# Expert rows fetched, added and stored instead of accumulated by the DMA, with two experts' weights loaded after the first gathers

## The chip, the cores and the metric

The kernel runs on one core of a Trainium2 chip. The metric is the device time of one execution in microseconds (us), as the median of several runs. A profile is taken of one execution, and its times count from the start of that execution's span.

## The reference, cut to what matters

The program computes one layer of a streaming encoder for 1024 frames of a prompt and 64 frames of a sample (1088 rows of 1024 fp32 values). After two kinds of attention and an output projection, every row goes through a mixture of 32 experts, of which each row uses two, both out of one of four groups:

```python
x = x + merge_branches(o_a, o_b, gate_logit, w_pa, w_pb, w_o)
hx = rmsnorm(x, g_ffn)
grp = argmax(hx @ w_rg + b_rg)
top_p, top_i = top_k(softmax(fine_sel), 2)
expert = grp * 8 + top_i
hid = silu(hx @ w1[e]) * (hx @ w3[e]) * combine[e]
x = x + sum_e hid @ w2[e]
```

The weights of an expert are w1 and w3 (1024 x 128) and w2 (128 x 1024), all fp32: three loads of 512 KB.

## The kernel before

The program is one long list of instructions for each engine. The last quarter of it is what matters here: the output projection (`out` and `out_tile`, nine tiles of 128 rows) and the experts (`moe`).

**Output projection.** Each tile of rows is multiplied by w_o and added to the input rows in a tile `y`. The result goes to the output `out_y` in DRAM (line 927), its normalized copy goes to a DRAM buffer `hxd` (line 934), and a router (`route`, `place`) works out which slot of which expert each row takes. An expert has 96 slots (`CAP`). Slots that no row takes get a row number far outside the buffer. The router's last result is `ptab`, a table of slots by experts, held in PSUM.

**Experts.** `moe` takes them in an order in which the group changes at every step (`expert`), so two experts that can share a row are at least four steps apart. For each expert it

- gathers up to 96 normalized rows from `hxd` by an indirect DMA on GpSimd's queue (`gather`, line 1066); an unfilled slot moves nothing,
- transposes them on TensorE (`turn`), multiplies by w1 and w3 and applies silu (`hidden`),
- multiplies by w2 into two PSUM halves, which ScalarE (left half, line 1112) and VectorE (right half, line 1114) scale by the row's weight into a tile `ot`, and adds `ot` onto the rows of `out_y` by an indirect DMA that accumulates in DRAM (`scatter`, line 1115). All 96 slots are moved there: an unfilled slot adds to one of 4 x 96 spare rows behind the real ones (line 1128 works out their numbers).

The gathers run up to `XG` = 3 experts ahead, the transposes two, `hidden` one.

**Weights.** `prefetch` (line 1054) issues the loads on SyncE's queue as soon as three free 4 KB-wide buffers (`units`) are there, at most `PF` = 3 loads in flight. There are 37 such buffers, 12 experts' worth. Seven experts' weights are loaded during the output projection, as tiles of the projection come free. After it, 16 more units are free, 8 called "r" and 8 called "u":

```python
self.free.extend(("r" * 8 + "u" * 8)[:NU0])
self.prefetch()
self.drain()
self.close("rp")
self.mp = self.open("mp", 1)
self.free.extend(("r" * 8 + "u" * 8)[NU0:])
```

With `NU0` = 8 the eight r units are handed out before the router's work drains; with the rest `moe` starts at step `E0` = -1, where it calls `prefetch` again. `HOLD_G` = -1 makes the first load that is issued there wait for the third gather. Later loads follow as experts finish.

**End.** `overflow` counts, after the last expert, how many experts have more than 96 rows (lines 1167 to 1184), and all engines branch on that number. With these inputs no expert has.

**Order.** TensorE's order is the order of the code. The order on the other engines, and on SyncE's and GpSimd's queues, is set by a scheduler.

Of the kernel before, what the change touches and what calls it, by code (L numbers as in the profile page):

```python
# [9 lines left out]
F32 = mybir.dt.float32  # L10
F32R = mybir.dt.float32r
BF = mybir.dt.bfloat16
I32 = mybir.dt.int32
U32 = mybir.dt.uint32
AF = mybir.ActivationFunctionType
OP = mybir.AluOpType
# [3 lines left out]
D = 1024  # L20
NTOK = 1088
NT = 9
NEG = -1e30
BIG = 1.0e6
CAP = 96
NOV = 22
EPS = 1e-6
NBIG, NSMALL = 4, 4
O_TURN, O_LOG, O_RANK, O_TAB = 3, 4, 7, 3
SA, SB, PTA, PTB, NORM_POOL, D_NORM, ATT0, ATT1, WPOOL, WR, SS, WO_EVERY, PF, SQ, V_POOL, RC_ACT, KT, NX, NN, NU0, E0, YB = 4, 3, 2, 1, 2, 0, 2, 26, 0, 4, 1, 3.5, 3, 2, 2, 2, 1, 10, 1, 8, -1, 3  # L30
PA, PF2, HOLD_G, HELD, WARM0, XG, OT, HXB = 8, 2, -1, 1, 11, 3, 2, 1
FIRST, GRP0 = 0, 4
WARM = 6, 3, 0, 2, 14
S_LOAD, S_H, S_H2, S_W, S_V, S_EVERY, GB = 4.5, 1.5, 6.5, 5.0, 3, 24, 2
# [8 lines left out]
def rows(i):  # L43
    return 128 if i < 8 else 64


class K:
# [1033 lines left out]
    def hidden(self, u, xT):  # L1081
# [16 lines left out]
        nc.vector.tensor_tensor(hl, t, hh.bitcast(F32), op=OP.subtract)  # L1098
        return (hh, wh), (hh, wl), (hl, wh)

    def scatter(self, parts, idx_r, wcol):

        nc = self.nc
        ot = self.mp.tile([128, D], F32, name="ot", bufs=OT)
        for hf in range(2):
            sl = slice(512 * hf, 512 * hf + 512)
            po = self.pp.tile([128, 512], F32, name="big", bufs=NBIG)
            for j, (a, b) in enumerate(parts):
                self.mm(po[:CAP], a, b[:, sl], start=(j == 0), stop=(j == 2))
            o = ot[:CAP, sl]  # L1110
            if hf == 0:
                nc.scalar.activation(o, po[:CAP], AF.Copy, scale=wcol)  # L1112
            else:
                nc.vector.tensor_scalar(o, po[:CAP], wcol, None, op0=OP.mult)  # L1114
        return nc.gpsimd.indirect_dma_start(out=self.O["y"], out_offset=bass.IndirectOffsetOnAxis(ap=idx_r, axis=0),  # L1115
                                     in_=ot[:CAP], in_offset=None, bounds_check=NTOK + 4 * CAP - 1, compute_op=OP.add)

    def moe(self):
        nc = self.nc

        t = self.mp.tile([CAP, 32], F32, name="t2")
        ti = self.mp.tile([CAP, 2, 32], I32, name="ti")
        tw = self.mp.tile([CAP, 32], F32, name="tw")
        self.placed = nc.vector.tensor_scalar(ti[:, 0], self.ptab[:, 0], BIG, None, op0=OP.add)
        nc.scalar.activation(tw, self.ptab[:, 1], AF.Copy, scale=0.5)
        for j in range(4):
            g = slice(8 * j, 8 * j + 8)
            nc.vector.tensor_scalar(t[:, g], self.ptab[:, 2, g], self.spare_b[:CAP, j:j + 1],
                                    self.spare[:CAP, j:j + 1], op0=OP.mult, op1=OP.add)
        nc.vector.tensor_tensor(ti[:, 1], self.ptab[:, 0], t, op=OP.add)  # L1130

        self.xgs = xgs = self.y[-XG:]
        xT, parts, sc = {}, {}, []
        for e in range(-XG, 32):
            if e + XG < 32:
                x = self.expert(e + XG)
                g = self.gather(ti[:, 0, x:x + 1], xgs[e % XG])
                if e == HOLD_G:
                    self.hold = g
            if e == E0:  # L1140
                self.prefetch()
            for d in (1, 2) if e < 0 else (2, 1):
                if d == 1 and 0 <= e + 1 < 32:
                    parts[e + 1] = self.hidden(self.ew[e + 1], xT.pop(e + 1))
                if d == 2 and 0 <= e + 2 < 32:
                    xT[e + 2] = self.turn(xgs[(e + 2) % XG])
            if e >= 0:
                x = self.expert(e)
                st = self.scatter(parts.pop(e), ti[:, 1, x:x + 1], tw[:, x:x + 1])
                for y in self.sy if e < 4 else sc[-4:-3]:  # L1150
                    self.after(st, y)
                for y in sc[-3:]:
                    self.tc.declare_no_dep(st.ins, y.ins, reason="a frame has one group; rows of another")
                sc.append(st)
                self.free.extend(self.which[e])
                self.prefetch()

    def overflow(self):

        nc, tc, I = self.nc, self.tc, self.I  # L1160
        V = nc.vector
        p = self.mp

        def T(name, *shape, dt=F32):
            return p.tile([128, *shape], dt, name=name, bufs=1)
        self.placed = None
        pc = self.pp.tile([128, 32], F32, name="small", bufs=NSMALL)
        for j in range(2):
            self.mm(pc, self.onesb, self.ohs[:, j], start=(j == 0), stop=(j == 1))
        nov = T("nov", 32)  # L1170
        V.tensor_scalar(nov, pc, float(CAP), None, op0=OP.is_gt)
        for m in range(2, (NTOK - 1) // CAP + 1):
            V.scalar_tensor_tensor(nov, pc, float(CAP * m), nov, op0=OP.is_gt, op1=OP.add)  # L1173
        inc = [T("inc0", 32), T("inc1", 32)]
        V.tensor_copy(inc[0], nov)
        a = 0
        for d in (1, 2, 4, 8, 16):
            V.tensor_copy(inc[1 - a][:, :d], inc[a][:, :d])  # L1178
            V.tensor_tensor(inc[1 - a][:, d:], inc[a][:, d:], inc[a][:, :32 - d], op=OP.add)  # L1179
            a = 1 - a  # L1180
        inc = inc[a]
        tot = T("tot", 1, dt=I32)
        V.tensor_copy(tot, inc[:, 31:32])
        val = nc.values_load(tot[0:1, 0:1], min_val=0, max_val=NOV)
        with tc.If(val > 0):
            ovb = T("ovb", 32)
            V.tensor_tensor(ovb, inc, nov, op=OP.subtract)
            fill = T("ofill", NOV, 3)
            V.memset(fill, 0.0)
# [1 line left out]
            for i in range(NT):  # L1191
                n = rows(i)
                for j in range(2):
                    jk, b, m, r = T("ojk", 32), T("ob", 1), T("om", 1), T("orow", 1, dt=I32)
                    V.scalar_tensor_tensor(jk[:n], self.ie[:n], self.ep[:n, i, j, 0:1], ovb[:n],
                                           op0=OP.is_equal, op1=OP.mult, accum_out=b[:n])
                    pos = self.ep[:n, i, j, 1:2]
                    V.tensor_scalar(m[:n], pos, float(CAP), BIG, op0=OP.is_lt, op1=OP.mult)
                    V.tensor_tensor(m[:n], m[:n], pos, op=OP.add)
                    V.tensor_scalar(b[:n], b[:n], float(CAP), -float(CAP), op0=OP.mult, op1=OP.add)  # L1200
                    V.tensor_tensor(r[:n], b[:n], m[:n], op=OP.add)
                    nc.gpsimd.indirect_dma_start(
                        out=self.otable, out_offset=bass.IndirectOffsetOnAxis(ap=r[:n, 0:1], axis=0),
                        in_=self.ent[:n, i, j, :], in_offset=None, bounds_check=CAP * NOV - 1, oob_is_err=False)
# [3 lines left out]
            w3v = I["w3"][0].rearrange("e (p k) f -> (e p) (k f)", k=8)  # L1208
            w2v = I["w2"][0].rearrange("e f d -> (e f) d")
            with tc.For_i(0, val):  # L1210
                jk, e, ix = T("ojk", 32), T("oe", 2), T("oix", 2, dt=I32)
                V.tensor_scalar(jk, inc, num, None, op0=OP.is_le)
                V.tensor_reduce(e[:, 0:1], jk, axis=mybir.AxisListType.X, op=OP.add)
                V.tensor_copy(e[:, 1:2], num)
# [4 lines left out]
                for dst, src in zip(u, (w1v, w3v, w2v)):  # L1219
                    nc.gpsimd.indirect_dma_start(  # L1220
                        out=dst, out_offset=None, in_=src,
                        in_offset=bass.IndirectOffsetOnAxis(ap=ix[:, 0:1], axis=0), bounds_check=4095, oob_is_err=False)
                ob = T("otb", 3)
                nc.gpsimd.indirect_dma_start(
                    out=ob[:CAP], out_offset=None, in_=self.otable,
                    in_offset=bass.IndirectOffsetOnAxis(ap=ix[:CAP, 1:2], axis=0), bounds_check=CAP * NOV - 1, oob_is_err=False)
                ti, tr, tw = T("oti", 2, dt=I32), T("otr", 1), T("otw", 1)
# [189 lines left out]
```

## Time and profile before

| what | value |
| --- | --- |
| median of 3 runs | 1236.51 us (1236.01 to 1240.26) |
| the profiled execution | 1243.3 us, of which the span is 1241.5 us |
| busy in the span | PE 1187.3 us (96%), VectorE 801.4 us (65%), ScalarE 741.1 us (60%), GpSimd 319.2 us (26%) |
| moved by DMA | 156.32 MB, of which the queue of GpSimd (q0) 21.50 MB |

The profiled execution is 6.8 us longer than the median of the runs. PE is TensorE's matmuls, DVE is VectorE, ACT is ScalarE, POOL is GpSimd, SP is SyncE. The DMA share is the mean busy share of the core's 16 DMA engines; it can pass 1, as packets of two queues overlap on an engine. q1 is the queue of SyncE, q10 that of ScalarE, q0 that of GpSimd's indirect DMAs.

### The profile page before, as it was taken

How to read it: one execution, taken by the hardware profiler on the slowest of the kernel's cores; microseconds unless marked ns; L12 is line 12 of the kernel's file. 1: busy time of each engine (PE TensorE's matmuls, PEld its weight loads, DVE VectorE, ACT ScalarE, POOL GpSimd, SP SyncE). 2: the span in 40 equal slices, each digit the busy share in tenths (PEclk: the TensorE clock that was granted, in tenths of full speed). 3: DMA queues.
4: the chain of work that ended last, by engine and by line, in shares of the span. 5: the costliest groups of instructions: out<-in, count | busy, mean ns of one | idle time of the engine just before them, and what ended most of it. 6: DMA issues, size and time to landing. Idle time of an engine off the chain costs nothing. (4 is left out here: it accounts for less than half of the span.)

```text
span 1241.5 us, 22308 instructions
## 1 busy us (share of the span) xinstructions
PE 1187.3 (96%) x7605; PEld 1105.8 (89%) x7605; DVE 801.4 (65%) x2476; ACT 741.1 (60%) x1730; POOL 319.2 (26%) x469
## 2 busy tenths in 40 slices
PE   8999999999999999999999899999999989999884
PEld 6899999999889999999898899999888859999773
DVE  6768776767498888978467685229544445655443
ACT  5789998989598988988456444324233323333221
POOL 2644435352434334100000000000000024554321
PEclk9999999999999999999999899999999989999887
DMA  8113121312222231411234333214674479999995
GB/s 283 56 55 92 33 74 50 90 48 78 58 82 56 70 67 40 88 44 43 67 89 131 88 89 99 59 45 143 230 264 154 136 215 268 287 282 282 283 280 136
DMA packets 102539, 156.32 MB, mean 126 GB/s; under 512 B 13581, under 2 KB 77941, under 8 KB 102389
## 3 DMA queue, kind: packets, MB, share of 16 engines
q1 hardware_dynamic: 92789, 124.43, 33.1%
q0 software_dynamic: 7168, 21.50, 8.0%
q10 hardware_dynamic: 2464, 8.91, 1.8%
q8 instruction: 61, 1.00, 0.3%
q14 instruction: 57, 0.47, 0.1%
HBM read 122.08 MB, written 38.23 MB: 129 GB/s over the span
## 5 line engine op out<-in xcount | busy, mean ns | idle before, releaser
L83 PE MATMUL big<-w,hTh 128*128 128x384 f32 (+1 forms) x1152 | 322.8, 351 | 0.9 <-ACT raw L380 0.3
L83 PEld LDWEIGHTS big<-w,hTh 128*128 128x128 f32 x1152 | 203.8, 188 | 6.6 <-ACT w L227 1.3
L83 PE MATMUL big<-hTh,w 128*128 128x384 f32 (+1 forms) x768 | 204.9, 335 | 0.0
L83 PE MATMUL big<-w,hTl 128*128 128x384 f32 (+1 forms) x512 | 172.8, 337 | 1.3 <-DVE hTl L194 1.3
L83 PEld LDWEIGHTS big<-hTh,w 128*128 128x128 f32 x768 | 138.5, 189 | 1.3
L83 PE MATMUL big<-hTl,w 128*128 128x384 f32 (+1 forms) x384 | 126.4, 329 | 0.0
L636 DVE TENSOR_TENSOR PT<-small,PT 128x512 fp32r<-128x512 f32 (+2 forms) x192 | 98.7, 519 | 16.4 <-ACT PT L635 15.0
L536 ACT ACTIVATE S<-S,mns 128x640 f32<-128x640 f32 (+7 forms) x128 | 94.1, 735 | 23.2 <-DVE mns L598 21.9
L83 PE MATMUL big<-ath,w 128*128 128x384 f32 (+1 forms) x384 | 100.2, 337 | 0.0
L540 ACT ACTIVATE S<-S,rc 128x640 f32<-128x640 f32 (+7 forms) x128 | 93.8, 736 | 7.8 <-DVE rc L538 6.9
L83 PEld LDWEIGHTS big<-w,hTl 128*128 128x128 f32 x512 | 96.5, 188 | 1.8 <-DVE hTl L194 1.6
L95 PE MATMUL small<-ident,S 128*128 128x128 f32 x528 | 89.4, 273 | 3.4 <-ACT S L540 3.0
L635 ACT CAST PT<-small 128x512 fp32r<-128x512 f32 (+2 forms) x192 | 84.5, 447 | 11.3 <-PE small L83 4.8
L83 PE MATMUL small<-PT,v 128*128 128x256 f32 x608 | 83.5, 283 | 0.1
L83 PEld LDWEIGHTS small<-PT,v 128*128 128x128 f32 x608 | 79.5, 188 | 0.5 <-DVE PT L636 0.3
L411 POOL TENSOR_TENSOR ssr<-ssa,mhalf 128x8 f32<-128x8 f32 (+1 forms) x40 | 61.2, 1531 | 69.3 <-DVE ssa L410 53.5
L95 PEld LDWEIGHTS small<-ident,S 128*128 128x128 f32 x528 | 66.2, 140 | 11.4 <-ACT S L540 5.1
L83 PE MATMUL big<-wo,mh 128*128 128x512 f32 x288 | 75.9, 402 | 0.0
L83 PEld LDWEIGHTS big<-hTl,w 128*128 128x128 f32 x384 | 72.8, 190 | 0.1
L83 PEld LDWEIGHTS big<-ath,w 128*128 128x128 f32 x384 | 69.7, 192 | 1.5 <-issue 0.2
L1115 POOL DMA_INDIRECT out_y<-ot,ti x32 | 58.1, 1815 | 49.0 <-ACT ot L1112 14.0
L83 PE MATMUL big<-k,qh 128*128 128x320 f32 (+3 forms) x192 | 65.1, 342 | 4.3 <-DVE mns L598 4.0
(259 smaller groups left out, 2547.3 us busy)
## 6 DMA issues: line engine op xcount, KB each, us to landing
uo<-in_w SPq DMA_DIRECT2D x43, 512.0 KB
ux<-in_w SPq DMA_DIRECT2D x30, 512.0 KB
ur<-in_w SPq DMA_DIRECT2D x23, 512.0 KB
wraw<-in_w_pair SPq DMA_DIRECT2D x56, 192.0 KB
wraw<-in_w_in SPq DMA_DIRECT2D x32, 192.0 KB
atd<-at SPq DMA_DIRECT2D x32, 128.0 KB
bias<-ccd SPq DMA_DIRECT2D x8, 512.0 KB
y<-in_x_prompt SPq DMA_DIRECT2D x8, 512.0 KB
```

The costliest lines, as they stand in the source:

```text
L83: self.nc.tensor.matmul(out, a, b, start=start, stop=stop)
L95: self.nc.tensor.transpose(out, a, ident)
L411: nc.gpsimd.tensor_tensor(r[:n, :4 * c], a[:n, :4 * c], self.mhalf[:n, :4 * c], op=OP.pow)
L536: nc.scalar.activation(S[:nq, :n], S[:nq, :n], AF.Exp, bias=mn[:nq], scale=-1.0, accum_out=sm[:nq])
L540: nc.scalar.activation(S[:nq, :n], S[:nq, :n], AF.Copy, scale=rc[:nq])
L635: nc.scalar.copy(hi, pt[:, sr, :])
L636: nc.vector.tensor_tensor(PT[:, 1, sr, 128 * j:128 * j + 128], pt[:, sr, :], hi.bitcast(F32), op=OP.subtract)
L1115: return nc.gpsimd.indirect_dma_start(out=self.O["y"], out_offset=bass.IndirectOffsetOnAxis(ap=idx_r, axis=0), in_=ot[:CAP], in_offset=Non ...
```

## The change

The accumulating DMA is replaced by three steps. `fetch` gathers the rows of `out_y` into `ot`. `put` has VectorE compute product times weight plus `ot` for both halves. A plain indirect DMA then stores `ot` back. The fetch takes the same row numbers as the gather, and so does the store, so unfilled slots move nothing. There are three `ot` tiles instead of two, set to zero once. A fetch waits for the store four experts earlier (same group). `NU0` goes from 8 to 0. The counting moves from the end into the loop, behind expert 6 (`COUNT`), and its small tiles lie in space of the router's weights.

```diff
-... KT, NX, NN, NU0, E0, YB = ... 1, 10, 1, 8, -1, 3
-PA, PF2, HOLD_G, HELD, WARM0, XG, OT, HXB = 8, 2, -1, 1, 11, 3, 2, 1
+... KT, NX, NN, NU0, E0, YB = ... 1, 10, 1, 0, -1, 3
+PA, PF2, HOLD_G, HELD, WARM0, XG, OT, HXB, COUNT = 8, 2, -1, 1, 11, 3, 3, 1, 6
...
+    def last(self, parts, hf):
+        po = self.pp.tile([128, 512], F32, name="big", bufs=NBIG)
+        for j, (a, b) in enumerate(parts):
+            self.mm(po[:CAP], a, b[:, 512 * hf:512 * hf + 512], start=(j == 0), stop=(j == 2))
+        return po
+    def fetch(self, idx_t, ot):
+        return self.nc.gpsimd.indirect_dma_start(out=ot[:CAP], out_offset=None, in_=self.O["y"],
+                                          in_offset=bass.IndirectOffsetOnAxis(ap=idx_t, axis=0),
+                                          bounds_check=NTOK - 1, oob_is_err=False)
+    def put(self, parts, idx_t, wcol, ot):
+        nc = self.nc
+        for hf in range(2):
+            o = ot[:CAP, 512 * hf:512 * hf + 512]
+            nc.vector.scalar_tensor_tensor(o, self.last(parts, hf)[:CAP], wcol, o, op0=OP.mult, op1=OP.add)
+        return nc.gpsimd.indirect_dma_start(out=self.O["y"], out_offset=bass.IndirectOffsetOnAxis(ap=idx_t, axis=0),
+                                     in_=ot[:CAP], in_offset=None, bounds_check=NTOK - 1, oob_is_err=False)
...
-            if hf == 0:
-                nc.scalar.activation(o, po[:CAP], AF.Copy, scale=wcol)
-            else:
-                nc.vector.tensor_scalar(o, po[:CAP], wcol, None, op0=OP.mult)
...
-        for j in range(4):
-            g = slice(8 * j, 8 * j + 8)
-            nc.vector.tensor_scalar(t[:, g], self.ptab[:, 2, g], self.spare_b[:CAP, j:j + 1],
-                                    self.spare[:CAP, j:j + 1], op0=OP.mult, op1=OP.add)
-        nc.vector.tensor_tensor(ti[:, 1], self.ptab[:, 0], t, op=OP.add)
+        self.ots = ots = [self.mp.tile([128, D], F32, name=f"ot{i}") for i in range(OT)]
+        for ot in ots:
+            nc.gpsimd.memset(ot, 0.0)
+        def fetch(e):
+            x = self.expert(e)
+            f = self.fetch(ti[:, x:x + 1], ots[e % OT])
+            for y in self.sy if e < 4 else sc[e - 4:e - 3]:
+                self.after(f, y)
+            for y in sc[max(e - 3, 0):]:
+                self.tc.declare_no_dep(f.ins, y.ins, reason="a frame has one group; rows of another")
+            fe.append(f)
...
+            if -1 <= e < 31:
+                fetch(e + 1)
...
-                st = self.scatter(parts.pop(e), ti[:, 1, x:x + 1], tw[:, x:x + 1])
-                for y in self.sy if e < 4 else sc[-4:-3]:
-                    self.after(st, y)
-                for y in sc[-3:]:
+                st = self.put(parts.pop(e), ti[:, x:x + 1], tw[:, x:x + 1], ots[e % OT])
+                for y in sc[-3:] + fe[e + 1:]:
...
+            if e == COUNT:
+                self.count()
```

How the order moves, at three places. In the rows, a name in brackets is a semaphore that is waited for: DMASW2 is at these places the third gather, DMAHW0 to 7 are DMAs of SyncE's and ScalarE's queues. First SyncE's queue at the seam between the output projection and the experts, before:

```order
L882 DMA out_y<-y 96x1024 [waits DMAHW5_49,DMAHW3_49,DVE_49]
L1054 DMA ur<-in_w 128x1024 [waits DMAHW0_49,PE_49]
L1054 DMA ur<-in_w 128x1024 [waits DMAHW6_49,DMAHW1_49,PE_49]
L1054 DMA ur<-in_w 128x1024 [waits DMAHW2_49,PE_49]
L1054 DMA ur<-in_w 128x1024 [waits DMAHW4_49,DMAHW1_49,PE_49]
L1054 DMA ur<-in_w 128x1024 [waits DMAHW5_49,DMAHW2_49,PE_49]
L1054 DMA ur<-in_w 128x1024 [waits DMAHW7_49,DMAHW4_49,PE_49]
L1054 DMA uo<-in_w 128x1024 [waits DMAHW7_49,DMAHW0_49]
L1054 DMA ur<-in_w 128x1024 [waits DMASW2_49,PE_49]
```

and with the change:

```order
L882 DMA out_y<-y 96x1024 [waits DMAHW5_49,DMAHW3_49,DVE_49]
L1054 DMA ur<-in_w 128x1024 [waits DMAHW2_49,DMASW2_49,PE_49]
L1054 DMA ur<-in_w 128x1024 [waits DMAHW6_49,DMAHW3_49,PE_49]
L1054 DMA ur<-in_w 128x1024 [waits DMAHW4_49,DMAHW1_49,PE_49]
L1054 DMA ur<-in_w 128x1024 [waits DMAHW5_49,DMAHW3_49,PE_49]
L1054 DMA ur<-in_w 128x1024 [waits DMAHW6_49,DMAHW4_49,PE_49]
```

The wait for the third gather stood at the eighth load behind that store, and now stands at the first: seven loads that went ahead of it now come after it.

Second GpSimd's queue where the experts begin, with the change (before, the three gathers were the first of these):

```order
L1143 MEMSET ot_13244 128x1024 [waits Activation_49]
L1143 MEMSET ot_13245 128x1024
L1143 MEMSET ot_13246 128x1024 [waits DMAHW1_49,Activation_49]
L1066 DMA y<-hxd,ti 96x1024 [waits DMAHW4_49,DMAHW5_49,DMAHW3_49,DMAHW7_49,DMAHW2_49,DVE_49]
L1066 DMA y<-hxd,ti 96x1024 [waits DMAHW5_49]
L1066 DMA y<-hxd,ti 96x1024 [waits DMAHW0_49]
L1110 DMA ot_13244<-out_y,ti 96x1024 [waits DMAHW6_49,DMAHW3_49,Pool_49]
L1110 DMA ot_13245<-out_y,ti 96x1024 [waits Pool_49]
L1110 DMA ot_13246<-out_y,ti 96x1024 [waits Pool_49]
L1066 DMA y<-hxd,ti 96x1024 [waits DMASW0_49,PE_49]
```

Three memsets come in front of the first gather, and three fetches between the third gather and the fourth.

Third the same queue in the middle of the experts, where before a gather (L1066) and an accumulating scatter (L1115) took turns:

```order
L1120 DMA out_y<-ot_13244,ti 1472x1024 [waits DMASW0_49,DVE_49]
L1110 DMA ot_13244<-out_y,ti 96x1024 [waits DMASW5_49,DMASW1_49]
L1066 DMA y<-hxd,ti 96x1024 [waits PE_49]
L1120 DMA out_y<-ot_13245,ti 1472x1024 [waits DMASW3_49,DVE_49]
L1110 DMA ot_13245<-out_y,ti 96x1024 [waits DMASW4_49,DMASW0_49]
L1066 DMA y<-hxd,ti 96x1024 [waits PE_49]
```

Each expert now has three DMAs there: its store, the fetch for the expert three steps later (which waits for the store before this one to have landed), and a gather.

## Rows read from the trace of the kernel before

**Rows 1.** The page, part 2: busy tenths of the DMA engines, 40 slices of 31 us.
```profile
DMA  8113121312222231411234333214674479999995
```

**Rows 2.** Stretches of 10 us: engines' busy us, PE clock, DMA share, GB/s.
```profile
1100.00:1110.00 10.00, 10.00 (x84) 9.49 (x83) 6.44 (x13) 3.93 (x7) 4.62 (x4) 1.00 1.04 292
1150.00:1160.00 10.00, 6.86 (x51) 5.99 (x50) 4.55 (x10) 1.47 (x3) 2.42 (x2) 0.96 1.03 298
```

**Rows 3.** The chain that ended last, from the first gathers on: start, us, what.
```profile
1017.00 7.40 DMA y<-hxd,ti
...
1030.60 0.86 PE small L95 x8
...
1036.44 0.86 PE small L95 x8
...
1140.30 7.95 DMA uo<-in_w
```

**Rows 4.** Timeline of SyncE's queue: start, us, loads issued.
```profile
976.59 0.34 SPq L1054 DMA_DIRECT2D uo<-in_w  x1
...
1000.78 10.28 SPq L1054 DMA_DIRECT2D ur<-in_w  x6
1016.50 0.33 SPq L1054 DMA_DIRECT2D uo<-in_w  x1
1024.46 0.80 SPq L1054 DMA_DIRECT2D ur<-in_w  x2
...
1213.06 0.33 SPq L1054 DMA_DIRECT2D ur<-in_w  x1
```

**Rows 5.** The page, part 3, queue of the indirect DMAs: packets, MB, share of 16 engines.
```profile
q0 software_dynamic: 7168, 21.50, 8.0%
```

**Rows 6.** DMA queues in the stretch 1200 to 1210 us.
```profile
q1 hardware_dynamic: 701, 2.54, 76.9%
q0 software_dynamic: 66, 0.26, 13.9%
```

**Rows 7.** DMA queue of SyncE in the stretch 886.4 to 899 us.
```profile
q1 hardware_dynamic: 1180, 4.28, 88.1%
```

**Rows 8.** Timeline around the first gathers: GpSimd's issues (idle before, its end), TensorE's first transposes.
```profile
1013.43 1.24 POOL L1066 DMA_INDIRECT y<-hxd,ti  x1 [3.55 <-DMA ur<-in_w]
...
1014.97 1.72 POOL L1066 DMA_INDIRECT y<-hxd,ti  x1 [0.30 <-issue]
...
1017.92 1.13 PE L95 MATMUL small<-ident,y 96*128 96x96 f32 x8 [1.05 <-DMA y<-hxd,ti]
```

**Rows 9.** GpSimd's instructions by form: count, busy us, mean ns, idle before.
```profile
L1115 POOL DMA_INDIRECT out_y<-ot,ti x32 | 58.1, 1815 | 49.0 <-ACT ot L1112 14.0 <-issue 8.9 <-ACT hT L1094 8.4
...
L1066 POOL DMA_INDIRECT y<-hxd,ti x32 | 33.8, 1057 | 77.8 <-PE small L95 40.5 <-DVE ot L1114 13.4 <-DVE hl L1098 9.9
...
L896 POOL MEMSET y<- 128x1024 f32 x1 | 1.0, 954 | 6.9 <-DMA hxd<-y 6.9
```

**Rows 10.** DMA queues in the stretch 1014.9 to 1016 us.
```profile
DMA packets 66, 0.07 MB, mean 63 GB/s; under 512 B 49, under 2 KB 49, under 8 KB 66
...
q0 software_dynamic: 59, 0.05, 32.2%
```

**Rows 11.** Queue of the indirect DMAs in the stretch 1016 to 1017 us.
```profile
q0 software_dynamic: 47, 0.18, 45.3%
```

**Rows 12.** The same queue in the stretch 1021.9 to 1024 us.
```profile
q0 software_dynamic: 99, 0.33, 62.0%
```

**Rows 13.** The same queue in the stretch 1024 to 1140 us.
```profile
q0 software_dynamic: 4303, 12.71, 48.5%
```

**Rows 14.** Queue of ScalarE's stores in the stretch 940 to 960 us.
```profile
q10 hardware_dynamic: 432, 1.57, 20.1%
```

**Rows 15.** VectorE's scaling of the right half, stretch 1000 to 1242 us.
```profile
L1114 DVE TENSOR_SCALAR ot<-big,tw 96x512 f32<-96x512 f32 x32 | 23.9, 746 | 25.7 <-DMA out_y<-ot,ti 18.4 <-PE big L83 5.1 <-PE small L95 2.2
```

**Rows 16.** Timeline of GpSimd at the end: the last accumulating scatter.
```profile
1227.14 1.40 POOL L1115 DMA_INDIRECT out_y<-ot,ti  x1 [0.88 <-issue]
```

More of the change, by code (lines that the diff above doesn't have):

```diff
@@ L29 @@
 O_TURN, O_LOG, O_RANK, O_TAB = 3, 4, 7, 3
-SA, SB, PTA, PTB, NORM_POOL, D_NORM, ATT0, ATT1, WPOOL, WR, SS, WO_EVERY, PF, SQ, V_POOL, RC_ACT, KT, NX, NN, NU0, E0, YB = 4, 3, 2, 1, 2, 0, 2, 26, 0, 4, 1, 3.5, 3, 2, 2, 2, 1, 10, 1, 8, -1, 3
-PA, PF2, HOLD_G, HELD, WARM0, XG, OT, HXB = 8, 2, -1, 1, 11, 3, 2, 1
+SA, SB, PTA, PTB, NORM_POOL, D_NORM, ATT0, ATT1, WPOOL, WR, SS, WO_EVERY, PF, SQ, V_POOL, RC_ACT, KT, NX, NN, NU0, E0, YB = 4, 3, 2, 1, 2, 0, 2, 26, 0, 4, 1, 3.5, 3, 2, 2, 2, 1, 10, 1, 0, -1, 3
+PA, PF2, HOLD_G, HELD, WARM0, XG, OT, HXB, COUNT = 8, 2, -1, 1, 11, 3, 3, 1, 6
 FIRST, GRP0 = 0, 4
@@ L1099, in hidden @@
         return (hh, wh), (hh, wl), (hl, wh)
+    def last(self, parts, hf):
[14 more added lines that the diff above has]
+                                     in_=ot[:CAP], in_offset=None, bounds_check=NTOK - 1, oob_is_err=False)
     def scatter(self, parts, idx_r, wcol):
         nc = self.nc
-        ot = self.mp.tile([128, D], F32, name="ot", bufs=OT)
+        ot = self.ots[0]
         for hf in range(2):
[L1106 to L1110, printed above, removed]
-            if hf == 0:
-                nc.scalar.activation(o, po[:CAP], AF.Copy, scale=wcol)
-            else:
-                nc.vector.tensor_scalar(o, po[:CAP], wcol, None, op0=OP.mult)
+            nc.vector.tensor_scalar(ot[:CAP, 512 * hf:512 * hf + 512], self.last(parts, hf)[:CAP], wcol, None, op0=OP.mult)
         return nc.gpsimd.indirect_dma_start(out=self.O["y"], out_offset=bass.IndirectOffsetOnAxis(ap=idx_r, axis=0),
@@ L1119, in moe @@
         nc = self.nc
-        t = self.mp.tile([CAP, 32], F32, name="t2")
-        ti = self.mp.tile([CAP, 2, 32], I32, name="ti")
+        ti = self.mp.tile([CAP, 32], I32, name="ti")
         tw = self.mp.tile([CAP, 32], F32, name="tw")
-        self.placed = nc.vector.tensor_scalar(ti[:, 0], self.ptab[:, 0], BIG, None, op0=OP.add)
+        self.placed = nc.vector.tensor_scalar(ti, self.ptab[:, 0], BIG, None, op0=OP.add)
         nc.scalar.activation(tw, self.ptab[:, 1], AF.Copy, scale=0.5)
-        for j in range(4):
-            g = slice(8 * j, 8 * j + 8)
-            nc.vector.tensor_scalar(t[:, g], self.ptab[:, 2, g], self.spare_b[:CAP, j:j + 1],
-                                    self.spare[:CAP, j:j + 1], op0=OP.mult, op1=OP.add)
-        nc.vector.tensor_tensor(ti[:, 1], self.ptab[:, 0], t, op=OP.add)
-        self.xgs = xgs = self.y[-XG:]
-        xT, parts, sc = {}, {}, []
+        self.xgs = xgs = self.y[-XG:]
+        self.ots = ots = [self.mp.tile([128, D], F32, name=f"ot{i}") for i in range(OT)]
+        for ot in ots:
+            nc.gpsimd.memset(ot, 0.0)
+        xT, parts, fe, sc = {}, {}, [], []
+        def fetch(e):
[6 more added lines that the diff above has]
+            fe.append(f)
         for e in range(-XG, 32):
@@ L1136, in moe @@
                 x = self.expert(e + XG)
-                g = self.gather(ti[:, 0, x:x + 1], xgs[e % XG])
+                g = self.gather(ti[:, x:x + 1], xgs[e % XG])
                 if e == HOLD_G:
@@ L1156, in moe, with count, T @@
                 self.prefetch()
+            if e == COUNT:
+                self.count()
+    def count(self):
+        V = self.nc.vector
+        p = self.mp
+        def T(name, *shape, dt=F32):
+            return p.tile([128, *shape], dt, name=name, bufs=1)
+        pc = self.pp.tile([128, 32], F32, name="small", bufs=NSMALL)
+        for j in range(2):
+            self.mm(pc, self.onesb, self.ohs[:, j], start=(j == 0), stop=(j == 1))
+        nov, *inc = [self.wr[:, j, 0:32] for j in range(3)]
+        self.nov = nov
+        V.tensor_scalar(nov, pc, float(CAP), None, op0=OP.is_gt)
+        for m in range(2, (NTOK - 1) // CAP + 1):
+            V.scalar_tensor_tensor(nov, pc, float(CAP * m), nov, op0=OP.is_gt, op1=OP.add)
+        V.tensor_copy(inc[0], nov)
+        a = 0
+        for d in (1, 2, 4, 8, 16):
+            V.tensor_copy(inc[1 - a][:, :d], inc[a][:, :d])
+            V.tensor_tensor(inc[1 - a][:, d:], inc[a][:, d:], inc[a][:, :32 - d], op=OP.add)
+            a = 1 - a
+        self.inc = inc[a]
+        self.tot = T("tot", 1, dt=I32)
+        V.tensor_copy(self.tot, self.inc[:, 31:32])
     def overflow(self):
@@ L1166, in overflow @@
         self.placed = None
[L1167 to L1184, printed above, removed]
+        nov, inc = self.nov, self.inc
+        val = nc.values_load(self.tot[0:1, 0:1], min_val=0, max_val=NOV)
         with tc.If(val > 0):
-            ovb = T("ovb", 32)
+            ovb = self.wr[:, 3, 0:32]
             V.tensor_tensor(ovb, inc, nov, op=OP.subtract)
@@ L1193, in overflow @@
                 for j in range(2):
-                    jk, b, m, r = T("ojk", 32), T("ob", 1), T("om", 1), T("orow", 1, dt=I32)
+                    jk, b, m, r = self.wr[:, 4, 0:32], T("ob", 1), T("om", 1), T("orow", 1, dt=I32)
                     V.scalar_tensor_tensor(jk[:n], self.ie[:n], self.ep[:n, i, j, 0:1], ovb[:n],
@@ L1210, in overflow @@
             with tc.For_i(0, val):
-                jk, e, ix = T("ojk", 32), T("oe", 2), T("oix", 2, dt=I32)
+                jk, e, ix = self.wr[:, 4, 0:32], T("oe", 2), T("oix", 2, dt=I32)
                 V.tensor_scalar(jk, inc, num, None, op0=OP.is_le)
```

## The prediction

> **What bounds the kernel now.** I read the page's slices first: the DMA engines are far from full until slice 33, and from slice 34 to 39 their share stands at 9 tenths [rows 1]. The change touches only this last stretch, so the rest of the views are of it. The stretches of 10 us show two phases: at 1100 us TensorE is busy all the time beside DMA engines at 1.04, and at 1150 us TensorE has only 6.86 us of 10 beside DMA engines just as full [rows 2]. The chain of waits says the same: two successive experts start their transposes at 1030.60 and 1036.44, so TensorE alone needs 5.84 us an expert, and at 1140.30 the chain leaves TensorE for a load of weights and goes from load to load [rows 3]. So the experts begin on a stock of loaded weights, eat it up, and from 1140 us on go at the pace of the DMA engines. The end is set by when the last weights arrive, hence by all the DMA work that must be done between the first gathers and there.
>
> The queue of loads shows the stock. 21 loads (seven experts) are issued up to 976.59; seven more, six at 1000.78 and one at 1016.50, go out before the third gather has landed; the other 68 follow from 1024.46 to 1213.06 [rows 4]. That is 188.6 us for 67 intervals, 2.815 us a load and 8.45 us an expert, where TensorE needs 5.84.
>
> **The prices.** All are engine time per 4 KB packet: the share times 16 engines times the stretch, over the packets. A load costs 0.198 us late in the stage (76.9% of 160 us, 2.54 MB being 620 packets of 4 KB) [rows 6] and 0.170 where loads run nearly alone (88.1% of 201.6 us, 4.28 MB, 1045 packets) [rows 7]. A row that is accumulated costs 0.337 us (13.9% of 160 us, 66 packets; the last gather was long over) [rows 6]. A plain store to DRAM costs 0.168 (20.1% of 320 us, 1.57 MB, 383 packets) [rows 14]; the change's store of scattered rows isn't in the trace, and this is its nearest row. A gathered row, which is also the nearest row for a fetched one, has three readings: 0.169 (45.3% of 16 us, 43 rows) [rows 11], 0.26 (62.0% of 33.6 us, 0.33 MB, 80 rows) [rows 12], and 0.223 in the stage itself (48.5% of 1856 us is 900; 12.71 MB are 3103 rows; 19 scatters of 96 rows at 0.337 take 615 of it, which leaves 285 for 1279 rows) [rows 13]. I take 0.223, the one measured under the load that the fetch will meet.
>
> How rows lie on the engines matters as much. The bytes of the whole queue [rows 5] are 32 scatters of 96 rows (12.58 MB) and 8.92 MB of gathers, that is 2176 filled rows, 68 of 96 slots per expert. In the first microsecond of the first gather 49 of 66 packets are under 512 B [rows 10], and in the second only 4 of 47 are [rows 11]. If slots went round the engines in turn, each engine would reach its unfilled slots last. They come first, so whole engines hold nothing but unfilled slots: I conclude that slots go to the engines in blocks of six, and that the engines with the low slots carry six rows of every gather. Rows 11 fit: 45% of 16 engines is about seven busy at a time. A load is complete only when its share on the busiest engine is, so I cost the row DMAs by six rows on a busy engine, not by their mean.
>
> **The change, part by part.**
>
> *Seven loads later.* SyncE's queue now waits for the third gather ahead of seven loads that it used to issue before it. They took time in which the DMA engines have little else to do, and move into the stage that they bound. A load is eight packets on each engine: 8 x 0.198 = 1.58 us, times seven is **+11.1 us** (with 0.170: 9.5).
>
> *The gathers land earlier.* The third gather took 7.40 us from its issue at 1017.00 [rows 3] beside a load; the first, with almost no load left, let TensorE begin 4.5 us after its issue at 1013.43 [rows 8]. Three memsets of 0.954 us come ahead on GpSimd [rows 9]; it had been idle for 3.55 us before that first issue [rows 8], so they fit in there and end near 1012.8, and with the waits behind them I count 0.4 us. Issues of 1.06 us [rows 9] with 0.30 between [rows 8] put the third gather at 1013.83 + 2.72 = 1016.55 and its landing at 1021.05, so loads start **3.4 us** earlier than 1024.46 (bounds 0, if nothing in the landing was contention, and 6). TensorE's own start hangs on the first gather and moves by no more than the 0.4 us, which the stock of seven experts covers.
>
> *Fetch and store for accumulate.* On a busy engine an expert's scatter costs 6 x 0.337 = 2.02 us, its fetch and store 6 x (0.223 + 0.168) = 2.35, so +0.32 us, times 31 experts **+10.0 us**. With the lowest price of a fetched row it is 0, with 0.26 and a store at a load's 0.198 it is 6 x 0.121 x 31 = +22.5. If all engines shared the rows evenly, it would be (68 x 0.391 - 96 x 0.337) / 16 = -0.36 us an expert, -11.1 us.
>
> The Trainium skill, DMA: Bandwidth & Descriptors, section Anatomy of one DMA, prices a DMA of this queue by 2.0 us plus its bytes over 436 GB/s, whatever its operation. By that the 5.24 MB that the change adds (26.74 against 21.50) cost 12.0 us in place of the 10.0, and the sum below would be +18; the trace speaks against pricing by bytes alone, since an accumulated row takes twice a stored one [rows 6, 14].
>
> *VectorE, ScalarE, GpSimd.* VectorE takes the left half too, 0.746 us an expert [rows 15]; it is busy 6.44 us of 10 at the PE pace [rows 2], 3.8 us of 5.84, so it goes to 4.5 and stays hidden under TensorE, more so under the DMA pace; without that cover it would cost 0.75 us for the last expert alone. ScalarE loses as much. GpSimd's queue goes from 1.815 + 1.057 us of issue an expert to 1.815 + 2 x 1.057, with 0.3 us between [rows 9, 8]: 4.8 us. It also waits for the store before the last to land, behind it the next gather and the next store. At 8.45 us an expert there is room; the rival below prices its loss. The count's two dozen small operations move under the loop, and SyncE reads their result in the middle of its loads, with three in flight: nothing.
>
> *The end.* From the issue of the last scatter at 1227.14 to the span's end are 14.4 us [rows 16]. The last two scatters share the engines, 2 us each; two stores take 1 us each. The count no longer sits between the last VectorE operations. Together **-1.5 us** (0 to -3).
>
> *Sum:* 11.1 - 3.4 + 10.0 - 1.5 = **+16.2 us** on the profiled execution's 1243.3. That execution is 6.8 us over the median of the runs, so I put the sum on the median: 1236.5 + 16.2 = **1252.7 us**. With each term at its low end as long as busy engines decide, 9.5 - 6 + 0 - 3 = +0.5; at the high ends 11.1 - 0 + 22.5 - 0 = +33.6.
>
> **The rivals.**
>
> *Even engines (faster).* If work is shared evenly enough that the mean over 16 engines sets the pace, and a fetched row costs 0.169, an expert saves (96 x 0.337 - 68 x 0.337) / 16 = 0.59 us, 18.3 over 31: 11.1 - 3.4 - 18.3 - 1.5 = -12.1, **1224.4 us**. It decides once the saving per expert passes 0.20 us (6.2 us for the other terms). For it: the DMA share of 1.04 in the full stretch [rows 2] leaves little room for idle engines. Against it: rows 10 and 11. Chance 0.13.
>
> *A draw.* Even engines with the fetched row at 0.223 give 11.1 - 3.4 - 11.1 - 1.5 = -4.9 (1231.6); busy engines with a fetched row at 0.169 and loads 6 us earlier give 11.1 - 6 + 0 - 1.5 = +3.6 (1240.1). Around **1236 us**. For it: the cheap reading of rows 11 is the purest. Chance 0.19.
>
> *GpSimd's queue becomes the bound.* Between two stores stand the landing of the store before, a fetch and a gather. If a store takes L us to land, the queue turns in (L + 2.7) / 2 us an expert. It passes 8.45 only from L = 14.2; at 15.5 it is 9.1 us, and 32 experts from 1018 on [rows 8] end TensorE near 1309, where the last scatter was issued at 1227 [rows 16]: about **1318 us**. Against it: the slowest gather shown lands in 7.40 us. Chance 0.04.
>
> That the loads aren't moved after all is excluded by the order of SyncE's queue.
>
> **How the numbers follow.** A measurement of this kernel can tell about 0.5% (6.2 us) from no change. The forecast, slower by 6 to 32 us, has 0.64. With GpSimd's queue that makes slower 0.68, the draw is same 0.19, even engines faster 0.13. The busy-engine case alone spans 1240 to 1268. The range goes down into the other cases, to 1229, and up to 1268; it leaves out most of the even engines and GpSimd's rival.
>
> **What would show it.** Right: loads 22 on are issued from about 1021 us and none between 977 and there; TensorE's first long wait for a weight comes well before 1140, near 1100; the load pace in the stage is slower than 2.815 us, or equal with 75 loads after the seam; q0 moves 26.7 MB; the last load is issued some 15 us after 1213. Wrong: a load pace under 2.6 us (even engines), TensorE waiting for gathers or VectorE for fetches rather than for loads (GpSimd's queue), or a store that costs more than 0.2 us a row.

## The result, and the profile after

| | before | after |
| --- | --- | --- |
| median of 4 runs beside each other | 1238.05 us | 1272.29 us (1270.38 to 1276.38) |
| the profiled execution, its span | 1243.3, 1241.5 us | 1270.97, 1269.2 us |
| moved by GpSimd's queue q0 | 21.50 MB | 26.76 MB |
| loads issued after the gathers, first to last | 68 in 188.6 us | 75 in 222.1 us |

The changed kernel takes 1.0285 times as long (95% interval 1.0262 to 1.0307), 34 us more by the medians. The direction was forecast, the size was not: 16.2 us were, and 1272.3 lies above the range (1229 to 1268).

The page of the kernel after, parts 2 and 3 (for [rows 1, 5]):

```profile
DMA  8213030312222232210334323135844299999993
...
q0 software_dynamic: 10752, 26.76, 7.0%
```

SyncE's queue after (for [rows 4]; start, us, loads issued):

```profile
973.20 0.33 SPq L1054 DMA_DIRECT2D uo<-in_w  x1
...
1018.51 20.52 SPq L1054 DMA_DIRECT2D ur<-in_w  x8
...
1240.60 0.33 SPq L1054 DMA_DIRECT2D ur<-in_w  x1
```

No load goes out between 973 and 1018, the hole that the page's slice 32 shows, at 2 tenths. Then 75 loads need 222.1 us, 3.00 us a load where it was 2.815. The last one is issued 27.5 us later than before, and the spans differ by 27.7: the whole loss lies between the first and the last of these loads. From the last load to the end of the span are 28.6 us, before 28.4.

The stretch 1050 to 1140 before, then the same and two of 10 us after (for [rows 2]; the columns are busy us of PE, PE's weight loads, VectorE, ScalarE and GpSimd, then PE clock, DMA share, GB/s):

```profile
1050.00:1140.00 90.00, 90.00 (x715) 84.06 (x715) 55.39 (x108) 31.91 (x61) 47.12 (x32) 1.00 1.03 282
```

```profile
1050.00:1140.00 90.00, 79.68 (x597) 72.28 (x595) 51.55 (x119) 17.42 (x36) 37.81 (x37) 0.96 0.95 290
1100.00:1110.00 10.00, 8.83 (x70) 7.92 (x70) 4.14 (x8) 1.37 (x3) 4.19 (x5) 1.00 0.97 293
1150.00:1160.00 10.00, 10.00 (x80) 9.16 (x79) 8.27 (x19) 3.21 (x7) 4.52 (x4) 1.00 0.87 283
```

TensorE waits 10 us of these 90, where it waited for nothing before. And it doesn't wait for weights: its longest waits from 1019 to 1150 are for ScalarE, which in its turn waits for VectorE (second row, of the stretch 1010 to 1275; engine and line, what it waited for, us in total, times, longest):

```profile
PE big L83 <- ACT hh L1097: 9.8, 3, 6.9
```

```profile
ACT hh L1097 <- DVE hT L1096: 78.1, 21, 12.8
```

And yet the mean share of the DMA engines is lower than before (0.95 against 1.03, and 0.87 at 1150). Read alone, that looks as if the engines had room and something else held the work up. The chain after seems to say what (for [rows 3]; start, us, what):

```profile
1109.27 16.32 DMA ot<-out_y,ti
...
1128.56 11.94 DMA ot<-out_y,ti
...
1152.74 8.51 DMA ur<-in_w
```

Up to 1140 it runs through the landings of fetches, which the prediction had not on any path; from 1152 on it goes from load to load, as before. So two accounts were open. Either the new chain of store, fetch and addition turns too slowly, through GpSimd's and VectorE's queues, or some DMA engines are full while others are not, and everything that lands is late for that reason.

### The profile page after: what moved, and what is told of

The parts are those of the page before. It is cut to its first block, busy times and chain, and to the rows that moved or that the text cites. A ratio compares the mean times of both kernels' runs of the same rounds, so it can differ in the third digit from the quotient of the medians.

```text
span 1269.2 us, 22330 instructions
## 1 busy us (share of the span) xinstructions
PE 1196.4 (94%) x7605; PEld 1112.8 (88%) x7605; DVE 817.3 (64%) x2503; ACT 720.9 (57%) x1698; POOL 334.3 (26%) x504
## 3 DMA queue, kind: packets, MB, share of 16 engines
q0 software_dynamic: 10752, 26.76, 7.0%
## 5 line engine op out<-in xcount | busy, mean ns | idle before, releaser
L83 PE MATMUL small<-xT,uo 128*128 128x96 f32 x464 | 63.7, 300 | 9.3 <-DMA uo<-in_w 9.3
L83 PEld LDWEIGHTS small<-xT,uo 128*128 128x128 f32 x464 | 61.6, 215 | 10.6 <-DMA uo<-in_w 6.1
```

Source lines behind the costliest of these rows:

```text
L83: self.nc.tensor.matmul(out, a, b, start=start, stop=stop)
```

## The experiments

Eleven runs, each beside the kernel before; e9 is that kernel itself, and e10 is e2 again. Differences are of medians.

**The two halves of the change, each alone.** e1 is the changed kernel with the loads where they were; e2 is the kernel before with the loads deferred.

```diff
 e1, in the changed kernel; e2 has the reverse edit in the kernel before
-... NU0 ... = ... 0 ...
+... NU0 ... = ... 8 ...
```

> The changed kernel with eight units freed before the block is drained again (NU0 8), so that the loads are issued as before and only the plain fetch and store, VectorE's second half and the moved count are left of the change. Theory A (the sum on record: deferral +11.1 - 3.4, extra traffic +10.0, end -1.5) expects +8.5 on the kernel before, near 1246.5. Theory B (the fetch's landing is a wait that the sum did not have: fetch behind a store's landing on GpSimd's queue, VectorE behind the fetch; that is worth most of the 18 us that the sum missed) expects +20 to +27, 1258 to 1265. Theory C (the deferral was mis-sized, and holds the missing 18 us) expects +10 or less.

> The kernel before with NU0 0: the accumulating scatter stays, only the loads from number 22 on are held until the block is drained. Theory A: +11.1 - 3.4 and nothing at the end, +6 to +8, near 1245. Theory B: the same +6 to +11. Theory C: +20 or more, 1258. If the price of both parts simply adds, the difference from e1 and this one to the kernel before sum to the +34 of the change; a sum above +34 says that they share a wait, a sum below it that each makes the other worse.

e1: 1261.68 us, ratio 1.0195 (1.0162 to 1.0227), +23.9 us. e2: 1249.84 us, ratio 1.0112 (1.0086 to 1.0138), +12.0. They add up to 36 against the change's 34, so the halves are nearly independent. Theory A's sizes, +8.5 and +6 to +8, are too small for both, most for the plain stores, and theory C falls: the deferral doesn't hold the missing 18 us.

**Is it the landing?** e3 fetches two experts ahead, with four `ot` tiles and one weight buffer less (36 still hold twelve experts), so that the fetch has a whole further expert's time to land. The lines show the order alone.

```diff
-            if -1 <= e < 31:
-                fetch(e + 1)
+            if e == -1:
+                fetch(0)
+            if -1 <= e < 30:
+                fetch(e + 2)
```

> e1 with four ot tiles in place of three and each expert's fetch issued two experts ahead of its put in place of one; the 4 KB come from one weight unit (NX 9 in place of 10, which leaves 36 units, twelve whole experts as before). The same rows are fetched and stored, so the DMA engines move the same bytes. Theory B expects the waits of VectorE's L1119 for the fetch and of GpSimd's fetch for a store to go and the time to fall by 10 to 18 us below e1. Theory A (the fetch costs its DMA time, not its landing) expects no change from e1, within 2 us.

1265.16 us, ratio 1.0233 (1.0192 to 1.0274): not faster than e1. The waits stayed too. These rows are of the stretch 1010 to 1275, e1 first, then e3:

```profile
DVE ot L1119 <- DMA ot<-out_y,ti: 62.2, 21, 7.3
POOL ot L1110 <- DMA out_y<-ot,ti: 54.0, 23, 4.8
```

```profile
DVE ot L1119 <- DMA ot<-out_y,ti: 59.9, 24, 6.6
POOL ot L1110 <- DMA out_y<-ot,ti: 57.1, 21, 6.4
```

A fetch that is issued an expert earlier makes VectorE wait as long as before. Theory B falls in the form in which it was put. But e3 loosens only VectorE's half of it: on GpSimd's queue the fetch still waits for the same store as in e1 (57.1 us against 54.0). SyncE's queue in the kernel after answers for that half, in the stretch 1018 to 1241:

```profile
SPq L1054 <- DMA uo<-in_w: 77.4, 30, 4.6
SPq L1054 <- DMA ur<-in_w: 52.6, 18, 8.0
SPq L1054 <- DMA ux<-in_w: 50.1, 19, 4.2
SPq L1054 <- DMA y<-hxd,ti: 28.7, 1, 28.7
SPq L1054 <- PE small L95: 0.7, 3, 0.3
```

The 28.7 us are the first load's wait for the third gather. Then the loads waited 180.1 us for earlier loads, as at most three are in flight, and no more than 0.7 us for any line that frees a buffer (e1: 184.3 and 1.0). However late the fetches make TensorE, they keep no load back, and the end follows the last load by 28.6 us. The longer waits in the chain are where the delay shows, not where it is made.

**Do unfilled slots cost anything?** e4 leaves the kernel before as it is but adds filled rows alone (a second line, not shown, lets the DMA skip row numbers out of bounds).

```diff
-                st = self.scatter(parts.pop(e), ti[:, 1, x:x + 1], tw[:, x:x + 1])
+                st = self.scatter(parts.pop(e), ti[:, 0, x:x + 1], tw[:, x:x + 1])
```

> The kernel before, with the accumulating scatter given the index list of the gather, whose unfilled slots lie out of bounds and are skipped, in place of the list with spare rows: 2176 rows are added in place of 3072, and none of the loads moves. If the engines that carry six rows set the pace, and the unfilled slots lie on the last rows of each list, hence on the same engines whatever the expert, the busiest engines keep their rows: no change, within 2 us. If the sum of the traffic sets it, 896 rows less at 0.337 us over 16 engines give -19 us, 1219.

1234.66 us, ratio 0.9984 (0.9962 to 1.0007): no change, though q0 moves 17.84 MB in place of 21.50. The stretch 1050 to 1140, of a second profile of the kernel before (e9, below) and of e4:

```profile
1050.00:1140.00 90.00, 90.00 (x711) 83.84 (x710) 55.01 (x109) 31.53 (x61) 45.36 (x31) 1.00 1.02 286
```

```profile
1050.00:1140.00 90.00, 90.00 (x709) 83.72 (x709) 54.30 (x108) 31.52 (x61) 45.85 (x31) 1.00 0.93 272
```

The mean share falls by 0.09 and nothing is won in the whole. That is what whole engines that hold only unfilled slots would do: the work that is gone was not on the engines that decide. The low share of the changed kernel has the same reading, since its fetches and stores leave the same engines without rows.

**Rows spread over the engines.** The same rows, in other slots: consecutive entries of an expert go to consecutive blocks of six slots. The edit is one line, in three kernels: e5 is e1 with it, e6 is e4 with it, e7 the changed kernel with it.

```diff
-        nc.gpsimd.iota(self.slot, pattern=[[1, CAP]], ...
+        nc.gpsimd.iota(self.slot.rearrange("p (a b) -> p a b", b=CAP // 16), pattern=[[1, 16], [16, CAP // 16]], ...
```

> e1 with one line changed: the slots of an expert are numbered so that consecutive entries go to consecutive blocks of six slots, hence round the 16 DMA engines. 68 of 96 filled slots then put 4.25 rows on each engine in place of six on eleven of them and none on four; no byte is added or removed. Theory P (the busiest engines set the pace, with 24 weight packets and 18 rows an expert): 12.75 rows in place of 18, 5.25 x 0.217 us = 1.1 us an expert less over some 28 experts, so 25 to 32 us below e1, 1230 to 1237, as far as TensorE lets it. Theory B (landings and waits in GpSimd's and VectorE's queues) and a theory in which the mean of the engines sets the pace both expect e1's time within 4 us, 1258 to 1266.

> e4 (the kernel before, adding filled rows alone) with the same line changed. Theory P: 4.25 added and 4.25 gathered rows on each engine in place of six and six, 1.75 x (0.33 + 0.24) = 1.0 us an expert, 18 to 28 us below e4 as far as TensorE lets it, 1210 to 1220, and the fastest of all kernels so far. The mean theory: no change from e4, 1234 within 4.

> The changed kernel with the same line changed, its loads deferred as they are. Theory P: e5 plus the price of the deferral (+7.7 by the sum, +14 by e2), 1238 to 1250, below the kernel after by 25 to 35. The mean theory and theory B: 1272 within 4.

| kernel | median us | ratio to before | against the same kernel unspread |
| --- | --- | --- | --- |
| e5, plain stores alone | 1239.37 | 1.0017 (0.9998 to 1.0035) | -22.3 (e1) |
| e6, filled rows added | 1219.12 | 0.9860 (0.9823 to 0.9898) | -15.5 (e4) |
| e7, the whole change | 1251.25 | 1.0107 (1.0067 to 1.0147) | -21.0 (after) |

The kernel before took 1238.1 us beside the kernel after, 1237.8 beside e1 to e4 and 1237.3 beside e5 to e8, so the last column can be read across these sets. That the rows lie as meant is seen in the first packets of the first gather: of e4 from 1013.8 to 1014.9 and from there to 1015.9, and of e6 from 1010.9 to 1012 and from there to 1013 (up to 13 packets of a stretch are of loads):

```profile
DMA packets 67, 0.08 MB, mean 71 GB/s; under 512 B 48, under 2 KB 48, under 8 KB 67
DMA packets 46, 0.16 MB, mean 156 GB/s; under 512 B 8, under 2 KB 8, under 8 KB 46
```

```profile
DMA packets 43, 0.16 MB, mean 149 GB/s; under 512 B 3, under 2 KB 3, under 8 KB 43
DMA packets 82, 0.10 MB, mean 103 GB/s; under 512 B 57, under 2 KB 57, under 8 KB 82
```

In e4 the small packets come first, as in [rows 10, 11]; in e6 they come last, so each engine has rows to move before its unfilled slots.

Nothing but the numbering of the slots differs, no byte more or less is moved, and 15 to 22 us go, a little less than expected below the unspread kernel in each case. So the busiest DMA engines set the pace, and the changed kernel's extra traffic hurts because it lies on those that were full already. The stretch 1050 to 1140, of e1 and of e5:

```profile
1050.00:1140.00 90.00, 81.03 (x604) 71.72 (x604) 53.01 (x121) 18.97 (x39) 39.27 (x37) 0.98 0.93 278
```

```profile
1050.00:1140.00 90.00, 89.46 (x701) 82.54 (x700) 64.45 (x144) 23.68 (x47) 50.75 (x44) 1.00 1.03 316
```

With the rows spread, the same engines carry 316 GB/s in place of 278, their mean share goes to 1.03, and TensorE's waits there all but vanish. The waits for landings shrink with them, in the same stretch and order as above (e5):

```profile
POOL ot L1110 <- DMA out_y<-ot,ti: 29.6, 15, 5.0
DVE ot L1119 <- DMA ot<-out_y,ti: 27.7, 14, 6.3
```

e6 beats both kernels by more than a measurement's doubt. What stops it is TensorE, which it keeps busy past 1140, where the kernel before began to wait (compare [rows 2]):

```profile
1150.00:1160.00 10.00, 10.00 (x80) 9.22 (x79) 6.03 (x13) 3.68 (x8) 5.32 (x3) 1.00 1.02 302
```

**The fetch's price.** e8 is e1 without the fetch. It stores the bare product, and so leaves out the addition to what `out_y` holds.

```diff
-            nc.vector.scalar_tensor_tensor(o, self.last(parts, hf)[:CAP], wcol, o, op0=OP.mult, op1=OP.add)
+            nc.vector.tensor_scalar(o, self.last(parts, hf)[:CAP], wcol, None, op0=OP.mult)
...
-            if -1 <= e < 31:
-                fetch(e + 1)
...
```

> e1 without the fetch: VectorE multiplies alone and the product is stored, so that the addition to what y holds is left out, and 2176 rows fewer are moved. Six rows at 0.217 us over 28 experts are 36 us of a busy engine, and by their overlap (shares of 1.07) some 34 of time. Theory P: 28 to 36 us below e1, 1226 to 1234, near the kernel before, whose accumulated row (0.33) then equals about 1.5 plain rows. If the fetch costs only its 0.054 above half an accumulated row, as the sum on record has it by 0.223 + 0.168 - 0.337, the kernel without it lies 31 x 6 x 0.223 = 41 us below e1, 1220, as far as TensorE lets it.

1220.78 us, 40.9 below e1. TensorE is busy all the time in its stretches too:

```profile
1050.00:1140.00 90.00, 90.00 (x716) 83.92 (x716) 64.88 (x145) 23.31 (x45) 39.38 (x32) 1.00 0.94 292
1150.00:1160.00 10.00, 10.00 (x80) 9.22 (x79) 6.45 (x14) 2.83 (x6) 3.88 (x3) 1.00 0.88 281
```

So the fetch is worth at least 40.9 us, which over 31 experts of six rows is 0.220 us a row. The prediction's 0.223 agrees with that, but as TensorE bounds e8, a higher price is not excluded. The run takes the waits for the fetch away with its bytes and can't split them. Its queue holds gathers and stores alone; in the stretch 1050 to 1140:

```profile
q0 software_dynamic: 3446, 8.62, 31.1%
```

That is 448 us of the engines for 2104 rows, 0.213 us a row, gathered and stored rows together. With 0.223 for the gathered half, a stored row takes 0.203, where the prediction had 0.168.

**The deferral, once more.** e9 is the kernel before, unchanged, for a second profile; e10 is e2 again; e11 is e6 with `NU0` 0.

> The kernel before, unchanged, for a second profile of it: the first was of an execution 6.8 us above the median of its runs, and its SyncE queue already stood 3.0 us later than in e2 at 976.59 against 973.59, ahead of all that the change touches. If that is a matter of the single execution, the last load is issued near 1208 in place of 1213.06, and the deferral's price by last loads (1218.43 in e2) comes near the 12 of the medians. If the two profiles agree, the deferral costs 5 us by its profile, and the rest of its 12 us lies outside what the loads show.

> e2 once more, beside e9 on one chip, for a second profile and a second interval: 1.006 to 1.014 if the first stands. By the sum on record +7.7 is 1.0062. Seven loads at the pace that the stage has in the profile (2.7 to 2.8 us a load, not the 1.58 us of their own eight packets on an engine) would be +19 less the earlier start.

> e6 with the loads from number 22 on deferred (NU0 0). In e6 TensorE is busy 30.00 of 30 us in every stretch from 1020 to 1170, so if a deferred load costs time only where loads are what TensorE waits for, part of the price goes: +0 to +8 on e6, 1219 to 1227. If the deferral costs whatever the stage is bound by, +12 to +14 as in e2, 1231 to 1233.

e9 took 1237.97 us in its one run. e10: 1249.49 us, ratio 1.0079 (1.0051 to 1.0107), +11.1. e11: 1225.37 us, 6.3 above e6. SyncE's queue in e9, e2 and e10:

```profile
973.68 0.34 SPq L1054 DMA_DIRECT2D uo<-in_w  x1
...
1021.00 0.80 SPq L1054 DMA_DIRECT2D ur<-in_w  x2
...
1209.79 0.33 SPq L1054 DMA_DIRECT2D ur<-in_w  x1
```

```profile
1018.26 17.72 SPq L1054 DMA_DIRECT2D ur<-in_w  x8
...
1218.43 0.33 SPq L1054 DMA_DIRECT2D ur<-in_w  x1
```

```profile
1018.59 15.31 SPq L1054 DMA_DIRECT2D ur<-in_w  x8
...
1223.34 0.33 SPq L1054 DMA_DIRECT2D ur<-in_w  x1
```

The kernel before issues its 68 loads in 188.8 us in the second profile as in the first (188.6), but it starts 3.5 us earlier, 2.9 of which it had gained before anything that the change touches (973.68 against 976.59 [rows 4]). Against this profile the last load comes 8.6 us later in e2 and 13.6 in e10, around the 11 to 12 of the medians. The loads alone take 200.2 and 204.8 us for 75, so the seven cost 11.5 to 16.0; the earlier start gives back 2.4 to 2.7. In e11 half of the deferral's price is gone, as expected where TensorE is the bound for longer and the hole in the loads is partly covered.

## Why the prediction was wrong in size

**Right: what bounds the kernel, and that engines with low slots decide.** The prediction read from the small packets of the first gather [rows 10, 11] that slots go to the engines in blocks of six, and priced the rows by a busy engine. e4 to e7 bear it out. The rival of the even engines (1224.4 us) is answered by e5: even where the slots are spread, plain stores without the deferral give 1239.4, no faster than before.

**Wrong: "Fetch and store for accumulate", +10.0 us.** Measured alone: +23.9 (1.0195), 13.9 of the 18 us that were missed. The failed step is the size of this term, by a mix of prices. The accumulated and the fetched row were priced from the full stage (0.337 and 0.223), the stored row at 0.168 from ScalarE's stores at 940 to 960 us [rows 14], where the page's slice 31 has the DMA engines busy for 4 tenths [rows 1]. And the load's packets were held at 0.198, as if they did not feel what runs beside them. The queues in the stretch 1050 to 1140, of e9, of e1, and q1 of the first profile before (packets, MB, share of 16 engines):

```profile
q1 hardware_dynamic: 4203, 15.31, 51.1%
q0 software_dynamic: 3470, 10.27, 50.6%
```

```profile
q1 hardware_dynamic: 3925, 14.30, 52.8%
q0 software_dynamic: 4112, 10.60, 40.1%
```

```profile
q1 hardware_dynamic: 4081, 14.85, 51.1%
```

The price is the share of the 1440 us that 16 engines have in 90, over the bytes in packets of 4 KB. e1's rows (gathered, fetched and stored together) cost 577 / 2588 = 0.223 us, and its weight packets 760 / 3491 = 0.218, where before they cost 0.197 (736 / 3738, e9) or 0.203 (736 / 3625). With 0.223 for the store as well, the prediction's own term is 6 x (0.223 + 0.223 - 0.337) x 31 = +20.3 in place of +10.0, and with e8's 0.203 it is +16.6; a store over 0.2 us a row was one of the prediction's signs of being wrong. The weights add 68 x 8 x 0.021 = +11.4, or +8.2 by the first profile. Together these are 25 to 32 us, the 24 measured and more; the times of packets that overlap on an engine count twice (e9's two shares add to 1.02). How the miss splits between the two was not settled. The bound that the prediction had worked out for this term, +22.5 with 0.26 for the fetch and 0.198 for the store, came near in number, by other prices than the measured ones.

By the rule of the Trainium skill that the prediction set beside this term (DMA: Bandwidth & Descriptors, section Anatomy of one DMA) the added bytes cost 12.0 us; its fixed 2.0 us for each of the 32 more DMAs are not in that number. e1 took twice the 12.0, and e5 shows that no count of bytes or of DMAs can hold here: 22 us went with both unchanged.

**Too small: "Seven loads later" and "The gathers land earlier", +11.1 - 3.4 = +7.7.** Measured: +12.0 (e2, 1.0086 to 1.0138) and +11.1 (e10, 1.0051 to 1.0107; 7.7 is 1.0062 and lies in this one). The seven loads cost 11.5 to 16.0 by the queue, not 11.1, and the start moves by 2.4 to 2.7, not 3.4. The whole start did come 5.95 us earlier in the profile after (1018.51 against 1024.46), which looks like more than was forecast; but 3.4 of it stands already ahead of the change, at 973.20 against 976.59 [rows 4].

**Wrong and small: "The end", -1.5.** From the issue of the last store after to the end of the span it is 14.7 us, where [rows 16] gave 14.4:

```profile
1254.48 0.91 POOL L1120 DMA_INDIRECT out_y<-ot,ti  x1 [1.71 <-DVE ot L1119]
```

From the last load it is 28.6 us after, 28.7 in e1 (1234.69 to 1263.4), and 28.4 and 26.4 in the two profiles of the kernel before. Nothing was gained there.

**VectorE, ScalarE, GpSimd at nothing.** Here the prediction had the path wrong for the stretch up to 1140: the chain goes through landings of fetches, not through TensorE and weights. Its sign, a first long wait for a weight near 1100, did not come; the first load on the chain is that of 1152.74. The sign of the queue's rival did: VectorE waited for fetches. The rival's condition, a store's landing of 14.2 us, was reached as well; the three kinds of row DMA landed in 14.2 to 16.1 us (medians) in e1's stretch:

```profile
y<-hxd,ti POOLq DMA_INDIRECT x13, 16.1
out_y<-ot,ti POOLq DMA_INDIRECT x12, 14.2
ot<-out_y,ti POOLq DMA_INDIRECT x12, 14.8
```

The prediction had held 7.40 us against it, a landing beside a single load. Yet at 14.2 us that queue turns in (14.2 + 2.7) / 2 = 8.45 us an expert, and e1's loads needed 9.5 (67 intervals in 212.1 us, 1022.59 to 1234.69). The loads waited for loads and not for buffers, e3 loosened the fetch and won nothing, and e5 halved the waits by moving rows to idle engines. The queue was slow with the engines, not in their place, and the rival's 1318 us did not come.

With the measured sizes the sum is 24 + 12 = 36, near the 34 of the change. The high ends of the terms had given +33.6; the range stopped at 1268, which is +31.5.

## What to carry to other kernels

Price every term of a sum under the load in which it will run; a price from a quiet stretch beside one from a full stretch gives a difference that is no one's. Where an indirect DMA has unfilled slots, look at which DMA engines its filled ones fall to: a mean share below 1 (0.93 in e1) can hide engines that are full, and renumbering the slots can be worth more than removing bytes. A long landing in the chain of waits can be a symptom: look also at what the queue waits for whose last transfer the end follows, and try issuing the late one earlier.

## What the runs showed beyond the prediction

- Accumulating in DRAM was the cheaper way here even with the rows spread: 1219.1 us (e6) against 1239.4 (e5) for the same filled rows.
- A weight packet took 0.197 and 0.203 us beside accumulated rows (the two profiles of the kernel before) and 0.218 beside plain ones (e1), though the mean share of the engines was lower there.
- 3.66 MB less through q0 changed nothing that could be measured (e4), and no byte less changed 15 to 22 us (e5 to e7).
